# The opening of a hybrid decoder layer: the first tile's mean square and the factor of single tiles, written with fewer VectorE operations

## The chip, the cores and the metric

The kernel runs on one core of a Trainium2 chip. The time is device microseconds of one execution on that core; several executions are timed and their median is given. A profiled execution has a time of its own, and a span, which is the stretch from its first to its last instruction.

The engines are named as in the profile: PE (TensorE; PEld is its weight load), DVE (VectorE), ACT (ScalarE), POOL (GpSimd) and SP (SyncE, which mostly issues DMAs).

## The reference

One layer over 1024 tokens of width 1024, all in float32. What matters here is its first line, the RMS norm of the input, whose result feeds one wide projection:

```python
def rms_norm(x, w):
    xf = x.astype(jnp.float32)
    y = xf * lax.rsqrt(jnp.mean(xf * xf, axis=-1, keepdims=True) + EPS)
    return (y * w.astype(jnp.float32)).astype(x.dtype)

h = rms_norm(x, attn_norm_w[l])
proj = h @ w_in[l]                      # q, k, v, u, g
...                                     # differential attention, Conformer convolution, gated merge
x = x + (g_a * y_a + g_b * y_b) @ w_out[l]
h = rms_norm(x, ffn_norm_w[l])
gt, up = jnp.split(h @ w_gate_up[l], 2, axis=-1)
x = x + (jax.nn.silu(gt) * up) @ w_down[l]
```

For each token the norm needs one factor, 1/sqrt(mean of squares + 1e-6).

## The kernel before, in words

The tokens lie in eight tiles of 128 (`xt0` to `xt7`), one token to a partition. Every matrix product is made of three float32r products (high by high, low by high, high by low), so each operand is split into a high part by ACT (`split_hi`, line 120) and a low part by DVE (`split_lo`, line 125). The output of the norm is turned by PE (`turn_x`, line 724) and split into `hT_hi` and `hT_lo`, which stay for the whole first half of the kernel. The first products are those of the value projection (line 1110), for which a weight block `wraw` is loaded at the start and split into `vwh` and `vwl`.

The opening is written out by hand: a list of steps (line 1124 on), each of which is held in its place on DVE, ACT and PE by `in_order`. The steps are, in order: dummy products that keep PE busy, the squares of tile 0, its factor (`roots`), the spreading of the norm's gain over the partitions (`spread_weights`, PE line 212 and the two ACT copies of line 213), the scaling of tile 0 (`norm`, line 714), one more dummy product, the split of the first weight block, the turn of tile 0, the first products of tile 0, then squares, factor and scaling of tile 1, then those of tiles 2 and 3 together, and so on in pairs.

Tile 0 comes in two halves of 512 columns, the first by a DMA of the SP queue and the second by one of the ACT queue (line 202). Its squares are made in two places: ACT squares and sums the first half (line 699), DVE the second (line 700), and DVE adds the two sums (line 703). `rstd_of` (line 682) makes mean plus epsilon from the sum. `rsq` makes the factor: ACT takes the square root `t` of `v` (line 652), DVE its reciprocal `r` (line 653), and four DVE operations refine it by one Newton step, r(1.5 - 0.5 v r r) (lines 654 to 657). All of these are on one number per partition. Tile 1's factor is made alone as well; tiles 2 to 7 go in pairs, and the attention's norms, 16 numbers at a time, use the same function.

The small tiles come out of a pool named `sm`, which keeps a place per tag in the order in which tags first occur. The pools that are opened after it (the x tiles, the value splits, the attention's and the output projection's tiles of the left side of the memory) lie behind it.

Of the kernel before, what the change touches and what calls it, by code (L numbers as in the profile page):

```python
# [10 lines left out]
F32 = mybir.dt.float32  # L11
F32R = mybir.dt.float32r
AF = mybir.ActivationFunctionType
ALU = mybir.AluOpType
AX = mybir.AxisListType

P = 128
S = 1024
D = 1024
# [7 lines left out]
EPS = 1e-6  # L27
# [30 lines left out]
def kernel(  # L58
# [28 lines left out]
    dve, act, pool, pe = nc.vector, nc.scalar, nc.gpsimd, nc.tensor  # L87
# [11 lines left out]
    sm = ctx.enter_context(tc.tile_pool(name="sm", bufs=4))  # L99
# [12 lines left out]
    def nm(s):  # L112
        uid[0] += 1
        return f"{s}_{uid[0]}"
# [529 lines left out]
    def rsq(v, n, fast):  # L644

        r = sm.tile([P, 16], F32, tag="r", name=nm("r"))[:, :n]
        t = sm.tile([P, 16], F32, tag="t", name=nm("t"))[:, :n]
        if fast:
            act.activation(t, v, AF.Ln)
            act.activation(r, t, AF.Exp, scale=-0.5)  # L650
        else:
            act.activation(t, v, AF.Sqrt)
            dve.reciprocal(r, t)
        dve.tensor_tensor(t, r, r, op=ALU.mult)
        dve.scalar_tensor_tensor(t, v, 3.0e38, t, op0=ALU.min, op1=ALU.mult)
        dve.tensor_scalar(t, t, -0.5, 1.5, op0=ALU.mult, op1=ALU.add)
        dve.tensor_tensor(r, r, t, op=ALU.mult)
        return r
# [21 lines left out]
    def rstd_of(ss, n, scale, fast=False):  # L680
        v = sm.tile([P, 16], F32, tag="v", name=nm("v"))[:, :n]
        dve.tensor_scalar(v, ss, scale, EPS, op0=ALU.mult, op1=ALU.add)
        return rsq(v, n, fast)
# [3 lines left out]
    sqs = {}  # L687

    def squares(tiles):

        ss = sqs[tiles] = sm.tile([P, 4], F32, tag="ssx", name=nm("ssx"), bufs=2)[:, : len(tiles)]
        for j, i in enumerate(tiles):
            junk = ap.tile([P, D], F32, tag="junk", name=nm("xj"), bufs=1)
            src = xts[i]
            if i:
                act.activation(junk[:], src[:], AF.Square, accum_out=ss[:, j : j + 1])
            else:
                s2 = sm.tile([P, 1], F32, tag="ss", name=nm("ss"), bufs=1)
                act.activation(junk[:, :512], src[:, :512], AF.Square, accum_out=ss[:, j : j + 1])
                dve.tensor_tensor_reduce(  # L700
                    junk[:, 512:], src[:, 512:], src[:, 512:], 1.0, 0.0, ALU.mult, ALU.add, accum_out=s2[:]
                )
                dve.tensor_tensor(ss, ss, s2[:], op=ALU.add)

    def roots(tiles):

        r = rstd_of(sqs.pop(tiles), len(tiles), 1.0 / D)
        for j, i in enumerate(tiles):
            rx[i] = r[:, j : j + 1]

# [373 lines left out]
    def opening():  # L1084
# [35 lines left out]
        def turn_low(i):  # L1120
# [3 lines left out]
        steps(  # L1124
            lambda: keep_busy(3),
            lambda: squares((0,)),
            lambda: [xload(i, nc.scalar) for i in (2, 3)],
            lambda: roots((0,)),
            lambda: spread_weights(0),
            lambda: spread_weights(1),  # L1130
# [8 lines left out]
            lambda: low_x(0),  # L1139
            lambda: v_tile(0),  # L1140
            lambda: squares((1,)),
            lambda: roots((1,)),
            lambda: norm(1),
            lambda: squares((2, 3)),
            lambda: roots((2, 3)),
            lambda: turn_x(1),
            lambda: low_x(1),
# [88 lines left out]
    n = 0  # L1236
# [235 lines left out]
    n = len(steps)  # L1472
# [205 lines left out]
    for c in range(NE, NKT):  # L1678
        with after(mean_hi if c == NE else None), after(first_gates if c == NE else None):
            w = ws.next()  # L1680
# [465 lines left out]
```

## Time and profile before

| what | value |
|---|---|
| median of 3 runs | 1724.92 us (1724.23 to 1725.0) |
| profiled execution | 1724.03 us, span 1722.3 us |
| PE busy | 1713.7 us of the span |
| DVE busy | 1274.9 us |
| ACT busy | 873.3 us |
| POOL busy | 221.1 us |
| granted PE clock | 1.00 of full speed |
| start of the first product of the projection (line 1110) | 9.97 us into the span |

The profile's page gives shares over the whole span. The change lies in the first 17 us of it, so the timeline of the engines there says more: each of its rows has a start and a duration in us, the engine, the line of the kernel, what is written from what, the shape, how many instructions are merged in the row, and in brackets how long the engine had been idle and what released it. [...]

### The profile page before, as it was taken

To read this page: it belongs to the slowest core of one execution; us is meant where nothing else is said; L and a number is where in the kernel's file an instruction comes from. 1 tells how busy PE (TensorE), PEld (TensorE's weight loads), DVE (VectorE), ACT (ScalarE), POOL (GpSimd) and SP (SyncE) were. 2 spreads that over 40 slices of the span, in tenths; PEclk is the share of its full clock that TensorE was granted. 3 is DMA by queue.
4 is the path that set the end of the run, shared out by engine and by line. 5 is a ranking of instruction groups with operands and counts; after the bars stand their busy time and mean duration, and the time that the engine had idled before them with its cause. 6 is when DMAs were issued, how large, how long until landed. Compare 5 with 4: busy or idle time off the path is not lost.

```text
span 1722.3 us, 25855 instructions
## 1 busy us (share of the span) xinstructions
PE 1713.7 (100%) x9243; PEld 1478.0 (86%) x9243; DVE 1274.9 (74%) x2128; ACT 873.3 (51%) x1958; POOL 221.1 (13%) x211
## 2 busy tenths in 40 slices
PE   9999999999999999999999999999999999999999
PEld 7997889998998998988788888888888888888887
DVE  7675889898988987977577769966676666565544
ACT  5333335767877886856466325633333333333332
POOL 3997851000000000000000000000000000000000
PEclk9999999999999999999999999999999999999999
DMA  6344445436345445354873683244455445598663
GB/s 209 117 125 136 130 150 147 113 100 178 106 127 145 118 125 145 95 149 141 305 243 123 202 301 109 77 139 157 147 175 167 154 142 166 179 350 287 216 214 133
DMA packets 261347, 281.64 MB, mean 164 GB/s; under 512 B 16545, under 2 KB 181985, under 8 KB 261218
## 3 DMA queue, kind: packets, MB, share of 16 engines
q1 hardware_dynamic: 253584, 266.66, 48.3%
q0 software_dynamic: 6000, 10.43, 2.8%
q10 hardware_dynamic: 1634, 2.89, 0.5%
q8 instruction: 73, 1.20, 0.3%
q14 instruction: 56, 0.46, 0.1%
HBM read 181.84 MB, written 85.50 MB: 155 GB/s over the span
## 4 chain that ended last, share of the span: by engine, by line
PE 95%; DVE 2%; DMA 2%; ACT 1%; issue 0%; SPq 0%; DVEq 0%; ACTq 0%
PE acc L984 30%; PE pg L168 12%; PE acc L488 12%; PE pg L169 12%; PE pg L170 12%; PE wo L1861 3%; PE sc L1294 2%; PE sc L1293 2%; PE pT L1332 2%; DVE acc L594 1%; PE pg L1110 1%; PE pW L168 1%; PE pW L170 1%; PE pW L169 1%; PE pQ L819 1%; DMA room<-in_w_out_dram 1%
## 5 line engine op out<-in xcount | busy, mean ns | idle before, releaser
L594 DVE SCALAR_TENSOR_TENSOR acc<-u,cw,acc 128x1023 f32<-128x1023 f32 (+14 forms) x240 | 303.4, 1264 | 22.7 <-ACT acc L588 20.1
L168 PE MATMUL pg<-whi,hT_hi 128*128 128x256 f32 x704 | 199.3, 284 | 0.8 <-DVE v L125 0.8
L169 PE MATMUL pg<-wlo,hT_hi 128*128 128x256 f32 x704 | 199.9, 284 | 0.0
L170 PE MATMUL pg<-whi,hT_lo 128*128 128x256 f32 x704 | 199.9, 284 | 0.0
L125 DVE TENSOR_TENSOR wlo<-draw,whi 128x1024 fp32r<-128x1024 f32 x75 | 91.7, 1223 | 83.9 <-ACT whi L120 73.5
L120 ACT CAST whi<-draw 128x1024 fp32r<-128x1024 f32 x75 | 79.1, 1055 | 129.5 <-PE acc L488 112.7
L168 PEld LDWEIGHTS pg<-whi,hT_hi 128*128 128x128 f32 x704 | 133.8, 191 | 2.6 <-DVE v L125 1.0
L169 PEld LDWEIGHTS pg<-wlo,hT_hi 128*128 128x128 f32 x704 | 134.3, 191 | 1.7
L170 PEld LDWEIGHTS pg<-whi,hT_lo 128*128 128x128 f32 x704 | 134.3, 191 | 1.6
L120 ACT CAST whi<-wraw 128x1024 fp32r<-128x1024 f32 x90 | 94.6, 1052 | 67.2 <-PE pg L169 35.1
L488 PE MATMUL acc<-wlo,whi 128*128 128x512 f32 x308 | 119.8, 389 | 0.0
L488 PE MATMUL acc<-whi,wlo 128*128 128x512 f32 x308 | 119.8, 389 | 0.0
L168 PE MATMUL pg<-hT_hi,whi 128*128 128x512 f32 x288 | 114.5, 398 | 0.0
L169 PE MATMUL pg<-hT_lo,whi 128*128 128x512 f32 x288 | 113.9, 395 | 0.0
L170 PE MATMUL pg<-hT_hi,wlo 128*128 128x512 f32 x288 | 113.9, 395 | 0.0
L1300 ACT ACTIVATE E<-E,mn 128x640 f32<-128x640 f32 (+7 forms) x128 | 99.5, 777 | 26.6 <-DVE mn L1295 26.0
L120 ACT CAST whi<-s 128x1024 fp32r<-128x1024 f32 x54 | 56.8, 1053 | 105.2 <-PE acc L984 102.1
L125 DVE TENSOR_TENSOR wlo<-wraw,whi 128x1024 fp32r<-128x1024 f32 x75 | 93.2, 1246 | 16.3 <-ACT whi L120 15.8
L984 PE MATMUL acc<-h_hi,whi 128*128 128x512 f32 x240 | 93.4, 389 | 0.0
L984 PE MATMUL acc<-h_lo,whi 128*128 128x512 f32 x240 | 93.4, 389 | 0.0
L1295 DVE CUSTOM_DVE_ANT_0 E<-sc,tb 128x512 f32<-128x512 f32 (+3 forms) x128 | 74.1, 584 | 24.2 <-PE pT L1332 13.9
L984 PE MATMUL acc<-h_hi,wlo 128*128 128x512 f32 x240 | 90.1, 389 | 0.0
(372 smaller groups left out, 4593.1 us busy)
## 6 DMA issues: line engine op xcount, KB each, us to landing
wraw<-in_w_gate_up_dram SPq DMA_DIRECT2D x44, 512.0 KB, 4.7
wraw<-in_w_in_dram SPq DMA_DIRECT2D x38, 512.0 KB, 4.3
qs<-qs SPq DMA_DIRECT2D x96, 128.0 KB, 2.3
wd<-in_w_down_dram SPq DMA_DIRECT2D x44, 256.0 KB, 3.2
tdT<-wd SPq DMA_DIRECT2D x88, 128.0 KB, 4.5
draw<-sdS SPq DMA_DIRECT2D x44, 256.0 KB, 3.9
draw<-tdT SPq DMA_DIRECT2D x44, 256.0 KB, 3.5
wraw<-in_w_in_dram SPq DMA_DIRECT2D x32, 256.0 KB, 3.2
```

Of the source, the lines that this page charges most:

```text
L120: act.copy(dst, src)
L125: last_lo[0] = dve.tensor_tensor(dst, src, f32(hi), op=ALU.subtract).ins
L168: pe.matmul(o, lh, rh, start=start, stop=False)
L169: pe.matmul(o, lh, rl, start=False, stop=False)
L170: last_mm[0] = pe.matmul(o, ll, rh, start=False, stop=stop).ins
L488: m = pe.matmul(o[s_][i][:], l_[:, ts], r_[:, 512:], start=start and j + y_ == 0, stop=j == n - 1 and y_ == 2, skip_group_check=not start,)
L594: dve.scalar_tensor_tensor(a_, us[c][:, : S - n], cw[:, c, t : t + 1], a_, op0=ALU.mult, op1=ALU.add)
L984: last_mm[0] = pe.matmul(o[:], a_[x_][:, k, :], b_[y_][:, k, :], start=start and k + x_ + y_ == 0, stop=k == 3 and x_ == 1, skip_group_che ...
L1293: pe.matmul(o[:, :w], qh[:, qs], k, start=True, stop=False)
L1295: dve.tensor_tensor_reduce(e[:, ks], o[:, :w], tb[:, S - nk + c0 : S - nk + c0 + w], 1.0, mn[:, j : j + 1] if c0 else 3.0e38, ALU.add, ALU ...
L1300: act.activation(e[:, :nk], e[:, :nk], AF.Exp, bias=mn[:, j : j + 1], scale=-1.0, accum_out=l[:, j : j + 1])
L1861: last_mm[0] = pe.matmul(o[s_][i][:], A[u_], B[v_], start=start and j + y_ == 0, stop=j == 3 and y_ == 2, skip_group_check=not start,).ins
```

## The change

Two things are written with fewer DVE operations.

First, the mean square of tile 0. ACT's square now carries a scale of 1/sqrt(1024), so that its sum is a part of the mean; DVE adds epsilon to that; and the DVE operation that squares and sums the second half scales by 1/1024 and starts its sum from the value just made. What it leaves is `v` itself, the mean plus epsilon, so the addition of the two sums and the multiply-add of `rstd_of` are gone for this tile. The operation over the second half now reads the sum that ACT made of the first.

Second, the Newton step where one tile stands alone (tiles 0 and 1). A new small tile `w` holds -0.5 v; it is written between the issue of the square root and the reciprocal. Behind the reciprocal two operations are left: t = (r w) r and r = (t + 1.5) r.

```diff
@@ -650,7 +650,14 @@
         else:
             act.activation(t, v, AF.Sqrt)
+            if n == 1:
+                w = sm.tile([P, 1], F32, tag="w", name=nm("w"), bufs=1)
+                dve.tensor_scalar(w[:], v, 3.0e38, -0.5, op0=ALU.min, op1=ALU.mult)
             dve.reciprocal(r, t)
+            if n == 1:
+                dve.scalar_tensor_tensor(t, r, w[:], r, op0=ALU.mult, op1=ALU.mult)
+                dve.scalar_tensor_tensor(r, t, 1.5, r, op0=ALU.add, op1=ALU.mult)
+                return r
         dve.tensor_tensor(t, r, r, op=ALU.mult)
...
@@ -695,16 +702,18 @@
             else:
-                s2 = sm.tile([P, 1], F32, tag="ss", name=nm("ss"), bufs=1)
-                act.activation(junk[:, :512], src[:, :512], AF.Square, accum_out=ss[:, j : j + 1])
+                v = sm.tile([P, 16], F32, tag="v", name=nm("v"))[:, :1]
+                act.activation(junk[:, :512], src[:, :512], AF.Square, scale=D**-0.5, accum_out=ss[:, j : j + 1])
+                dve.tensor_scalar(ss, ss, EPS, None, op0=ALU.add)
                 dve.tensor_tensor_reduce(
-                    junk[:, 512:], src[:, 512:], src[:, 512:], 1.0, 0.0, ALU.mult, ALU.add, accum_out=s2[:]
+                    junk[:, 512:], src[:, 512:], src[:, 512:], 1.0 / D, ss, ALU.mult, ALU.add, accum_out=v
                 )
-                dve.tensor_tensor(ss, ss, s2[:], op=ALU.add)
+                sqs[tiles] = v

     def roots(tiles):

-        r = rstd_of(sqs.pop(tiles), len(tiles), 1.0 / D)
+        ss = sqs.pop(tiles)
+        r = rsq(ss, 1, False) if tiles == (0,) else rstd_of(ss, len(tiles), 1.0 / D)
```

On DVE the instructions of tile 0 stood like this before (`ss_350` is the sum of the second half, `ssx_348` that of the first, `xt_102` is tile 0; the two rows named ISA are one operation, the sum over the second half and the reading of its accumulator):

```order
L700 ISA xj_349,ss_350<-xt_102 128x512
L700 ISA ss_350 128x1
L703 TENSOR_TENSOR ssx_348<-ssx_348,ss_350 128x1
L682 TENSOR_SCALAR v_358<-ssx_348 128x1
L653 RECIPROCAL r_360<-t_361 128x1
L654 TENSOR_TENSOR t_361<-r_360 128x1
L655 SCALAR_TENSOR_TENSOR t_361<-v_358,t_361 128x1
L656 TENSOR_SCALAR t_361<-t_361 128x1
L657 TENSOR_TENSOR r_360<-r_360,t_361 128x1
L714 SCALAR_TENSOR_TENSOR xt_102<-xt_102,r_360,anw_b 128x512 x2
```

In the change they stand like this:

```order
L707 TENSOR_SCALAR ssx_348<-ssx_348 128x1
L708 ISA xj_349,v_350<-xt_102,ssx_348 128x512
L708 ISA v_350 128x1
L655 TENSOR_SCALAR w_361<-v_350 128x1
L656 RECIPROCAL r_358<-t_359 128x1
L658 SCALAR_TENSOR_TENSOR t_359<-r_358,w_361 128x1
L659 SCALAR_TENSOR_TENSOR r_358<-t_359,r_358 128x1
L723 SCALAR_TENSOR_TENSOR xt_102<-xt_102,r_358,anw_b 128x512 x2
```

Two small operations between the sum and the square root are gone, one has come ahead of the sum and one ahead of the reciprocal, and four behind the reciprocal have become two. For tile 1, alone too, `w` stands between the row of `v` and the reciprocal, and four operations become two in the same way. On DVE nothing else moves, and PE, ACT, POOL and SP have the same instructions in the same order as before.

One thing moves that is not an instruction. The tag "ss", under which the removed `s2` lay, is still used further on by `seen` (line 1183), so the pool `sm` keeps its place and gains one of 32 bytes per partition for `w`. In the built program everything that lies behind `sm` on the left side of the memory starts 32 bytes later: `xt0` at byte 164896 of its partition instead of 164864, and likewise the other x tiles, the splits of the value projection, the attention's tiles (`E`, `ph`, `pl`, `tb`, `early`) and the residual tiles `xa`. Before, these DMA targets started at multiples of 512 bytes. `hT_hi`, `hT_lo`, the weight tiles `wraw`, `whi`, `wlo` and everything on the right side of the memory stay where they were.

## The prediction

> **What bounds the kernel now.** I read the head of the page first, then the busy time by stretches (columns: length of the stretch, then each engine's busy time and instructions, clock, DMA share, GB/s).
>
> ```profile
> span 1722.3 us, 25855 instructions
> PE 1713.7 (100%) x9243; PEld 1478.0 (86%) x9243; DVE 1274.9 (74%) x2128; ACT 873.3 (51%) x1958; POOL 221.1 (13%) x211
> 0.00:16.00 16.00, 13.62 (x48) 8.83 (x48) 9.18 (x27) 10.30 (x19) 5.75 (x13) 1.00 0.81 279
> 16.00:60.00 44.00, 43.73 (x300) 39.86 (x299) 34.61 (x59) 19.06 (x34) 28.22 (x23) 1.00 0.43 127
> 812.00:825.00 13.00, 12.04 (x54) 8.92 (x53) 7.27 (x8) 10.02 (x23) 0.32 (x2) 1.00 0.71 218
> 1019.00:1024.00 5.00, 4.66 (x21) 3.56 (x20) 5.00 (x9) 1.33 (x5) 0.00 (x0) 1.00 1.05 406
> ```
>
> PE is idle for 8.6 us of the whole span (1722.3 - 1713.7). From 16 us on it is as good as full: 43.73 of the next 44 us. Only the first 16 us are not PE's: there it works on dummies and waits for the first normed tile. So what the opening gains reaches the end undiminished, if it still stands when PE becomes full at about 16 us, and nothing else in the kernel can gain. I therefore follow the opening instruction by instruction. DVE, tile 0:
>
> ```profile
> 4.84 0.69 DVE L700 CUSTOM_DVE_ANT_0 xj<-xt 128x512 f32<-128x512 f32 x1 [3.31 <-DMA xt<-in_x_dram]
> 5.46 0.08 DVE L700 DVE_READ_ACCUMULATOR2_ANT ss<- 128x1 f32 x1
> 5.65 0.16 DVE L703 TENSOR_TENSOR ssx<-ssx,ss 128x1 f32<-128x1 f32 x1
> 5.85 0.15 DVE L682 TENSOR_SCALAR v<-ssx 128x1 f32<-128x1 f32 x1
> 6.27 0.16 DVE L653 RECIPROCAL r<-t 128x1 f32<-128x1 f32 x1 [0.27 <-ACT t L652]
> 6.47 0.16 DVE L654 TENSOR_TENSOR t<-r 128x1 f32<-128x1 f32 x1
> 7.04 0.16 DVE L657 TENSOR_TENSOR r<-r,t 128x1 f32<-128x1 f32 x1
> 7.31 0.75 DVE L714 SCALAR_TENSOR_TENSOR xt<-xt,r,anw_b 128x512 f32<-128x512 f32 x1
> 7.98 0.74 DVE L714 SCALAR_TENSOR_TENSOR xt<-xt,r,anw_b 128x512 f32<-128x512 f32 x1
> ```
>
> The reader sees small operations of 0.16 us that follow each other at 0.20 us, since each needs the one before. What stands around them on ACT and PE:
>
> ```profile
> 3.60 0.63 ACT L699 ACTIVATE xj<-xt 128x512 f32<-128x512 f32 x1 [1.58 <-DMA xt<-in_x_dram]
> 4.14 0.19 ACT L699 ACTIVATION_READ_ACCUMULATOR xj<-xt 128x1 f32 x1
> 6.03 0.20 ACT L652 ACTIVATE t<-v 128x1 f32<-128x1 f32 x1 [1.71 <-DVE v L682]
> 5.75 1.06 PE L212 MATMUL pm<-anw_b,one 1*128 1x512 f32 x1
> 6.84 0.59 ACT L213 COPY anw_b<-pm 128x512 f32<-128x512 f32 x1
> 7.83 1.05 ACT L120 CAST vwh<-wraw 128x1024 fp32r<-128x1024 f32 x1 [0.40 <-DMA wraw<-in_w_in_dram]
> 8.21 1.94 PE L724 MATMUL px<-ident,xt 128*128 128x128 f32 x8 [0.65 <-DVE xt L714]
> 9.33 0.59 ACT L120 CAST hT_hi<-px 128x512 fp32r<-128x512 f32 x1 [0.45 <-PE px L724]
> 9.81 1.05 ACT L120 CAST vwh<-wraw 128x1024 fp32r<-128x1024 f32 x1
> ```
>
> **The change part by part.** *The epsilon ahead of the sum.* ACT's sum is read by 4.33 (4.14 + 0.19); the new addition, priced as the row at 5.85, ends at about 4.53 and is ready for its successor by about 4.6. DVE's half of the tile lands only at 4.84, so the addition is hidden by that DMA, with 0.2 us to spare. Were the cover gone, it would cost 0.2 us. *Between sum and root.* The accumulator is read by 5.54; the root started 0.03 us after the end of `v` (6.00 to 6.03), so it now starts at 5.57 and ends at 5.77. *`w`* takes the place that the addition had, 5.65 to 5.80, in DVE's idle time before the reciprocal, and is the last to let it go: reciprocal at 5.85, the two operations at 6.05 and 6.25, the scaling at 6.52 (0.27 behind, as from 7.04 to 7.31). That is 0.79 us earlier than 7.31.
>
> The sum and the first new operation read a per-partition number as an operand, which the trace shows only in the large rows: 0.75 with one (line 714) against 0.69 for the sum without. So 0.06 each, if size does not matter, or nothing: 0.67 to 0.79; I take 0.7, nearer neither end. ACT's scale I cost at nothing; its square ends 0.2 us clear anyway.
>
> *What catches the gain.* Three things stand on the path next. The second scaling needs the second ACT copy, which starts when PE ends its product (5.75 + 1.06 = 6.81) and ends at 7.43 as before; so it runs at about 7.47 instead of 7.98 and keeps 0.5. PE's first turn follows the first scaling, and its four transposes end at 8.6 instead of 9.3. But ACT's cast of the weight block waits for its DMA, not for us: it runs from 7.83 to 8.88 as before, and the cast of `hT_hi` comes behind it, at 8.88 instead of 9.33 (0.45), or 0.1 earlier if ACT overlaps the two as it does at 9.81. So about 0.5 us is left behind tile 0. ACT works without a gap from there to tile 1's squares, so all of them move by that. I take it that the second weight block and tiles 1 to 3 have landed by then; no wait shows when they do.
>
> Tile 1, and tiles 2 and 3:
>
> ```profile
> 10.94 2.38 POOL L1137 TENSOR_TENSOR vwl<-wraw,vwh 128x1024 fp32r<-128x1024 f32 x1 [9.64 <-ACT vwh L120]
> 12.43 0.15 DVE L682 TENSOR_SCALAR v<-ssx 128x1 f32<-128x1 f32 x1 [0.36 <-ACT xj L696]
> 12.85 0.16 DVE L653 RECIPROCAL r<-t 128x1 f32<-128x1 f32 x1 [0.27 <-ACT t L652]
> 13.05 0.29 DVE L654 TENSOR_TENSOR t<-r 128x1 f32<-128x1 f32 x1
> 13.95 0.75 DVE L714 SCALAR_TENSOR_TENSOR xt<-xt,r,anw_b 128x512 f32<-128x512 f32 x1
> 14.86 0.19 ACT L696 ACTIVATION_READ_ACCUMULATOR xj<-xt 128x1 f32 x1
> 15.28 0.16 DVE L682 TENSOR_SCALAR v<-ssx 128x2 f32<-128x2 f32 x1
> 15.59 1.17 ACT L120 CAST hT_hi<-px 128x512 fp32r<-128x512 f32 x2
> 16.21 1.35 PE L1110 MATMUL pg<-vwh,hT_hi 128*128 128x256 f32 x8
> ```
>
> Tile 1 has two operations fewer (0.39), one with the dearer operand: 0.33 to 0.39. The row of 0.29 ends with POOL's (13.34 and 13.32): the DVE operation was held by it. POOL starts behind ACT's second weight cast and moves by the same 0.5, so the first new operation is held about as long. Tile 1's scaling thus comes 0.5 + 0.35 = 0.85 earlier. Then the squares of tile 3 limit: they are read by 15.05, less 0.5 is 14.55, so `v` of the pair stands at 14.6 instead of 15.28, the root and the cast 0.65 earlier, and PE's row at 16.21 likewise. From there PE is full. **The sum** is 0.65 us by this way, 0.45 if only ACT's gap counts, 0.85 if squares and landings give way too. I take 0.6.
>
> Against the profiled execution that is 1724.03 - 0.6 = 1723.4 (1.7 us lie around its span). The median of the runs shown stands 0.9 above it, so I predict 1724.92 - 0.6 = 1724.3 us. A difference of 0.2% is 3.45 us, about what a measurement of this kernel can tell from no change; the gain is a sixth of that.
>
> *The memory that moves.* 32 bytes more in the small pool shift x tiles, `early` and `xa` off their multiples of 512. No row shows what a DMA pays for such a start in this memory. Three of these transfers lie on the chain that ended last (start, us):
>
> ```profile
> 1.31 3.51 DMA xt<-in_x_dram
> 812.34 7.69 DMA early<-a_d
> 1013.29 5.10 DMA xa<-in_x_dram
> wd<-in_w_down_dram SPq DMA_DIRECT2D x44, 256.0 KB, 3.2
> draw<-tdT SPq DMA_DIRECT2D x44, 256.0 KB, 3.5
> u<-u_d SPq DMA_DIRECT2D x8, 512.0 KB, 4.4
> tb<-t_d SPq DMA_DIRECT2D x8, 512.0 KB, 4.2
> ```
>
> They sum to 16.3 us, so each per cent costs 0.16 us. Bounds: `tb` reads rows 4604 bytes apart, whose starts in the source fall anywhere, and lands no later than the aligned `u` (4.2 against 4.4): nothing, or even a gain of 5% (0.8 us), which I leave aside as scatter. `draw` starts 256 bytes past a multiple of 512 and `wd` on one: 9% longer, 1.5 us. I take nothing, since `tb` is the nearer case, and keep 1.5 for the range.
>
> [...]
>
> **The rivals.** *Swallowed:* the weight block, the gain's copy or a landing of tiles 1 to 3 takes what the factor gives. For it: ACT's wait for `wraw` stands right there, and DMA is busy 0.81 of the first 16 us. Against it: ACT was idle 0.45 us before `hT_hi`. Time: 1724.9 less 0 to 0.3, 1724.7. *Serial sum, slower:* before, the two halves were squared side by side; now DVE's sum waits for ACT's. It has 0.2 us to spare only because the SP half lands 1.2 us ahead (3.60 and 4.84). If both landed at 4.84, ACT's sum would be read at 5.57, epsilon added at 5.77, and DVE would start at 5.88, 1.04 later, against 0.7 saved: 0.3 slower, 1725.2. It decides from a lead below some 0.3 us. *Moved memory, slower:* transfers to the shifted tiles take longer. It cancels the gain from 4% (0.65 us); at 9% the time is 1724.3 + 1.5 = 1725.8; for 0.2% it would take 25%, for which no row speaks. *It does more:* the full 0.85, 1724.0. *It does not do what it says* is excluded: the built order has the operations named.
>
> **How the numbers follow.** Forecast 0.52; swallowed 0.20; moved memory 0.13; serial sum 0.07; more 0.08. The range takes in the forecast, the larger gain with the scatter of the three runs (1724.0 less 0.7), and the moved memory's 1725.8: 1723.3 to 1725.8. All cases lie within 0.2%; I leave 0.05 for transfers that are far dearer than any row (slower) and 0.02 for the reverse.
>
> **What would show it.** In the profile after, tile 0's first scaling at 6.5 to 6.65, the second at 7.47, the cast of `hT_hi` right behind the weight cast, tile 1's scaling near 13.1 and PE's row of 16.21 at 15.5 to 15.8. Wrong I would be if DVE's sum started after 4.84 (or its DMA), if ACT waited for a landing between 8.9 and 14, or if PE showed new idle time near 812 or 1019 behind `early` or `xa`.

## The result and the profile after

The changed kernel takes 1727.41 us (median of 22 runs, 1726.16 to 1729.16) against 1724.64 us (22 runs, 1723.21 to 1725.64) for the kernel before: a ratio of 1.0017, 95% interval 1.0011 to 1.0022. It is slower by 2.8 us. That lies outside the predicted range and, by 0.7 us, inside the bound of 0.2%. Both profiled executions fit: 1727.22 us after, 1724.03 before. A ratio compares all runs of two kernels; it is not the quotient of the medians beside it.

The head of the page, then the busy time by stretches as shown of before:

```profile
span 1725.4 us, 25852 instructions
PE 1717.1 (100%) x9243; PEld 1478.0 (86%) x9243; DVE 1275.1 (74%) x2125; ACT 873.0 (51%) x1958; POOL 221.2 (13%) x211
0.00:16.00 16.00, 13.94 (x50) 9.41 (x51) 9.52 (x28) 10.83 (x20) 6.26 (x15) 1.00 0.86 292
16.00:60.00 44.00, 43.90 (x301) 40.08 (x301) 33.96 (x55) 19.14 (x33) 28.40 (x21) 1.00 0.43 123
812.00:825.00 13.00, 12.20 (x61) 9.36 (x61) 6.33 (x7) 9.85 (x22) 0.54 (x3) 1.00 0.78 246
1019.00:1024.00 5.00, 4.61 (x21) 3.48 (x19) 4.27 (x7) 0.32 (x2) 0.00 (x0) 1.00 1.05 402
```

The span is 3.1 us longer and PE is busy 3.4 us longer, with the same 9243 products. PE's idle time is 8.3 us where it was 8.6. The time went into PE's own work, not into a wait. The opening, meanwhile, did what was forecast. DVE in the timeline of after, with two rows of ACT and one of PE:

```profile
4.26 0.15 DVE L707 TENSOR_SCALAR ssx<-ssx 128x1 f32<-128x1 f32 x1 [2.74 <-ACT xj L706]
5.06 0.75 DVE L708 CUSTOM_DVE_ANT_0 xj<-xt,ssx 128x512 f32<-128x512 f32 x1 [0.64 <-DMA xt<-in_x_dram]
5.85 0.15 DVE L655 TENSOR_SCALAR w<-v 128x1 f32<-128x1 f32 x1
5.85 0.20 ACT L652 ACTIVATE t<-v 128x1 f32<-128x1 f32 x1 [1.62 <-DVE v L708]
6.09 0.16 DVE L656 RECIPROCAL r<-t 128x1 f32<-128x1 f32 x1
6.29 0.22 DVE L658 SCALAR_TENSOR_TENSOR t<-r,w 128x1 f32<-128x1 f32 x1
6.54 0.16 DVE L659 SCALAR_TENSOR_TENSOR r<-t,r 128x1 f32<-128x1 f32 x1
6.80 1.41 DVE L723 SCALAR_TENSOR_TENSOR xt<-xt,r,anw_b 128x512 f32<-128x512 f32 x2
8.82 0.58 ACT L120 CAST hT_hi<-px 128x512 fp32r<-128x512 f32 x1
13.06 1.41 DVE L723 SCALAR_TENSOR_TENSOR xt<-xt,r,anw_b 128x512 f32<-128x512 f32 x2
15.72 1.23 PE L1119 MATMUL pg<-vwh,hT_hi 128*128 128x256 f32 x8 [0.24 <-ACT hT_hi L120]
```

From the start of the sum to the first scaling it takes 1.74 us (6.80 - 5.06) where it took 2.47 (7.31 - 4.84): 0.73 saved. In this execution the tile's second half landed 0.22 us later than in the one of before.

Where the time is lost shows in the answer for the line of the products that are made from sums of quarters of their matrices (line 984 before, 993 after). They come in two stretches: a part of the wide projection from 110 to 250 us, and the feed-forward's first product from 1100 to 1520. PE is full there, in both kernels: busy 140.00 us of the 140 and 420.00 of the 420. The columns are count, duration in ns (least, median, greatest), and the start of the first and of the last of them in us. `T1h` to `T4l` are such sums of the normed input, high and low parts, 512 columns at a time, which PE multiplies by weights of 128 x 128 from `whi`, `wlo`, `sh` or `sl`. Before:

```profile
L984 PE MATMUL acc<-hT_hi,whi x83: 387/389/496, 112.0 to 245.9; 128*128 128x512 f32 x83
L984 PE MATMUL acc<-T1h,whi x28: 389/389/389, 116.8 to 238.8; 128*128 128x512 f32 x28
...
L984 PE MATMUL acc<-T4h,sh x80: 389/389/389, 1151.6 to 1513.1; 128*128 128x512 f32 x80
```

After:

```profile
L993 PE MATMUL acc<-hT_hi,whi x83: 387/389/499, 111.3 to 247.7; 128*128 128x512 f32 x83
L993 PE MATMUL acc<-T1h,whi x28: 393/396/399, 116.1 to 240.5; 128*128 128x512 f32 x28
...
L993 PE MATMUL acc<-T4h,sh x80: 392/395/396, 1153.0 to 1516.2; 128*128 128x512 f32 x80
```

The first of the 28 products `T1h` by `whi` starts 0.7 us earlier than before, the last 1.7 us later: 2.4 us are lost between them. Between the first and the last `T4h` by `sh` of the second stretch another 1.6 to 1.7 us go. Each such product lasts 395 to 396 ns where it lasted 389, and from the start of one to the start of the next it is about 234 ns where it was 227 (worked out from all starts in the traces). The products of `hT_hi` by `whi`, in between them, last 389 as before.

The kinds that pay are those of the first stretch with `T1` to `T4` (12 kinds of 28, 336 products: 336 x 7 ns = 2.35 us) and those of the second with `sh` and `sl` (3 kinds of 80: 240 x 7 ns = 1.68 us). That is 4.0 us less 0.7 gained at the start: 3.3, against 3.1 in the span.

Where these tiles lie in the built programs fits the pattern. The `T` tiles of the first stretch and the `sh`, `sl` of the second moved by 32 bytes (`T1h` from 172544 to 172576, `sh` from 135680 to 135712). `hT_hi`, `whi`, `wlo`, the `T` tiles of the second stretch and the `sh`, `sl` of the first are where they were. Of the products of 512 columns, the kinds that pay are exactly those with one operand that moved and one that did not.

### The profile page after: what moved, and what is told of

Same layout as the page of the kernel before. It is cut to its first block, busy times and chain, and to the rows that moved or that the text cites. A ratio compares the mean times of both kernels' runs of the same rounds, so it can differ in the third digit from the quotient of the medians.

```text
span 1725.4 us, 25852 instructions
## 1 busy us (share of the span) xinstructions
PE 1717.1 (100%) x9243; PEld 1478.0 (86%) x9243; DVE 1275.1 (74%) x2125; ACT 873.0 (51%) x1958; POOL 221.2 (13%) x211
## 4 chain that ended last, share of the span: by engine, by line
PE 94%; DMA 2%; DVE 2%; ACT 1%; issue 0%; SPq 0%; ACTq 0%
PE acc L993 30%; PE acc L488 12%; PE pg L168 12%; PE pg L169 12%; PE pg L170 12%; PE wo L1870 3%; PE sc L1303 2%; PE sc L1302 2%; PE pT L1341 2%; PE pg L1119 1%; DVE acc L594 1%; PE pW L168 1%; PE pW L170 1%; PE pW L169 1%; PE pQ L828 1%; DMA room<-in_w_out_dram 1%
## 5 line engine op out<-in xcount | busy, mean ns | idle before, releaser
L120 ACT CAST whi<-draw 128x1024 fp32r<-128x1024 f32 x75 | 79.1, 1055 | 129.6 <-PE acc L488 111.1
```

Source lines behind the costliest of these rows:

```text
L120: act.copy(dst, src)
```

## Experiments

The theory formed on this: a product of 512 columns takes about 7 ns longer when its two operands do not start at the same place within some block of memory. The rivals: the loss comes from the new operations or the new tile, or it comes from where one operand lies by itself, the moved tiles no longer starting at a multiple of 64 or 128. A pool's unused tile `pad_sm` lies ahead of the small tiles, so its size moves what lies behind without an instruction. The expectations name the theories by letters: A is the first, counted within 64 bytes; B says that any operand off a multiple of 64 costs; C that only multiples of 256 or 512 count, later that the distance within 256 does; D is that of the new operations.

**The move alone**: the kernel before, moved by 32 bytes.

```diff
-    sm.tile([P, 32], F32, name="pad_sm", bufs=1)
+    sm.tile([P, 40], F32, name="pad_sm", bufs=1)
```

> The kernel before with 32 bytes more in the small pool and no operation changed; every tile that the change moved now lies exactly where the change puts it. Theory A (the product's operands, moved by 32 bytes, cost about 7 ns in each product of 512 columns of lines 984): slower than before by 3.8 us, 1728.4 us, with the 12 groups of T products between 110 and 250 us and the three of sh and sl after 1100 us at 395 instead of 389 ns. Theory D (the new operations or their waits disturb what follows): as before, 1724.6 us.

Measured: 1727.9 us (11 runs) against 1724.24 (27 runs), ratio 1.0022 [1.0013, 1.0030]. The same two kinds of product:

```profile
L984 PE MATMUL acc<-T1h,whi x28: 393/396/399, 117.4 to 241.7; 128*128 128x512 f32 x28
...
L984 PE MATMUL acc<-T4h,sh x80: 392/395/396, 1153.5 to 1516.8; 128*128 128x512 f32 x80
```

The move costs 3.7 us without any change to an operation. The first stretch is 124.3 us long (241.7 - 117.4) where it was 122.0, the second 363.3 where it was 361.5.

**The operations alone**: the change, but `w` takes the place of the tag "ss", so that nothing behind it moves.

```diff
-                w = sm.tile([P, 1], F32, tag="w", name=nm("w"), bufs=1)
+                w = sm.tile([P, 1], F32, tag="ss", name=nm("w"), bufs=1)
```

> The change with w under the tag that s2 had, so that nothing in the memory moves. Theory A: the opening's gain alone, 0.7 us faster than before, 1723.9 us, and all T products at 389 ns. Theory D: as the change, 1727.4 us.

Measured: 1723.95 us (11 runs), ratio 1.0003 [0.9993, 1.0013]. All products with `T` tiles are back at 389 ns. So the loss of the change is the move. Whether the operations gain is not settled by this run: its median is 0.3 us below before, while two of its runs (1728.84 and 1731.79) raise the mean. In its profiled execution PE was 0.5 us ahead behind the opening and lost 0.9 us at 224 us, where it waited 0.59 us for the `wlo` that POOL makes; the change itself shows no such wait there.

**Moved by 64, 128 and 256 bytes.** The first is the change with `pad_sm` 32 bytes larger, the other two are the operations alone with it 128 and 256 bytes larger (64 and 96 floats).

```diff
-    sm.tile([P, 32], F32, name="pad_sm", bufs=1)
+    sm.tile([P, 96], F32, name="pad_sm", bufs=1)
```

> The change with another 32 bytes in the small pool, so that the moved tiles lie 64 bytes off their old places. If the place within 64 bytes counts (theories A and B): 1723.9 us, as without any move, T products at 389 ns. If multiples of 256 or 512 bytes count (theory C, the transfers or the products): as the change, 1727.4 us or more.

> The change's operations, w in the old tag, and the tiles behind the small pool moved by 128 bytes. Where weights and moving operand start 32 or 64 bytes apart within 256 a product of 512 columns took 4 to 7 ns more; 256 bytes apart (late T with whi, before) it took none. If only an offset of a full 256 counts as none: T products of the first part and late sh, sl products at 391 to 396 ns, 2 to 3.7 us slower than without the move, 1726 to 1727.5 us. If 128 is harmless already: 389 ns and 1723.9 us.

> The same with a move by 256 bytes. If the two operands' places within 256 bytes count: no cost, products at 389 ns, 1723.9 us as without the move. If multiples of 512 are needed: as the change, about 1727 us.

Measured: 64 bytes 1726.98 us, ratio 1.0015 [1.0007, 1.0024]; 128 bytes 1728.0 us against 1725.06, ratio 1.0012 [1.0002, 1.0022]; 256 bytes 1723.63 us, ratio 0.9988 [0.9978, 0.9997]. One run of before, of 1732.29 us, lowers the last two ratios; without it the means stand at 1.0016 and 0.9992. The same kinds, moved by 64 bytes:

```profile
L993 PE MATMUL acc<-T1h,whi x28: 388/394/398, 116.6 to 240.1; 128*128 128x512 f32 x28
...
L993 PE MATMUL acc<-T4h,sh x80: 393/396/398, 1152.6 to 1516.3; 128*128 128x512 f32 x80
```

Moved by 128:

```profile
L993 PE MATMUL acc<-T1h,whi x28: 387/394/398, 116.2 to 240.3; 128*128 128x512 f32 x28
...
L993 PE MATMUL acc<-T4h,sh x80: 392/394/404, 1151.8 to 1515.6; 128*128 128x512 f32 x80
```

Moved by 256:

```profile
L993 PE MATMUL acc<-T1h,whi x28: 389/389/389, 115.7 to 237.7; 128*128 128x512 f32 x28
...
L993 PE MATMUL acc<-T4h,sh x80: 389/389/389, 1151.0 to 1512.5; 128*128 128x512 f32 x80
```

A multiple of 64 or of 128 is not enough, and the theories that ask for no more than that fall. At 256 the cost is gone. The place within 256 bytes is what counts.

**Nearly the whole left side moved by 32**, in the kernel before: now `hT_hi`, `whi` and the first stretch's `T` tiles lie alike again, all 32 bytes off a multiple of 256, while the right side stays.

```diff
-    cst.tile([P, 16], F32, name="pad_left")
+    cst.tile([P, 24], F32, name="pad_left")
```

> The kernel before with 32 bytes more at the start of the left side of the memory: hT, the weight splits whi and wlo, and all that lies behind them move by 32 bytes together; the right side stays. Theory A (it counts that weights and moving operand start at different places within 64 bytes): T products of the first part, both operands moved, stay at 389 ns; products that take one operand from either side become 395 ns (aT with whi, late T1 to T3 with whi, late T4 with sh, mT with whi, early T4 with sh, about 1570 of them): 10 us slower, 1735 us. Theory B (any operand off a multiple of 64 bytes costs): all products of 512 columns on hT, h2, cT and the weight splits too, some 4700: 30 us slower, 1755 us.

Measured: 1736.12 us (5 runs, 1735.55 to 1737.21), ratio 1.0070 [1.0056, 1.0084]: 11.9 us slower. By the addresses in the built program 1620 products of 512 columns now have their operands 32 bytes apart; at 7 ns each that is 11.3 us. Products of the first stretch with `whi`, of which both operands moved, products of the second with `whi`, of which one did, and those of the output projections (`aTl` on the right side, `cT_lo` on the left):

```profile
L984 PE MATMUL acc<-T1h,whi x28: 389/389/396, 117.4 to 240.6; 128*128 128x512 f32 x28
...
L984 PE MATMUL acc<-T1h,whi x80: 395/396/397, 1139.0 to 1512.7; 128*128 128x512 f32 x80
...
L169 PE MATMUL pg<-aTl,whi x128: 392/395/497, 822.7 to 916.9; 128*128 128x512 f32 x128
L169 PE MATMUL pg<-cT_lo,whi x128: 389/389/395, 917.6 to 1004.5; 128*128 128x512 f32 x128
```

Where both operands moved, nothing is paid although neither starts at a multiple of 256 any more. Where one moved, the product pays: `T1h` by `whi` free in the first stretch and dear in the second, the mirror image of the change. `aTl` by `whi` lasted 389 before, and its 128 products took 92.3 us from first to last start (819.8 to 912.1) where they now take 94.2; `cT_lo` by `whi`, both moved, takes 86.9 us in both. So it is the distance of two operands that counts, not the place of either. Products of 256 columns with one operand moved (`vwh` by `hT_hi`) stayed at 117 to 120 ns from start to start.

**The unit matrix at a multiple of 256**, with the operations alone: it begins 192 bytes behind one in the kernel before and in the change (224 where the left side is moved by 32), and is the moving operand of all transposes.

```diff
+    neglam = cst.tile([P, 1], F32, name="neglam")
+    lsum = cst.tile([P, 2], F32, name="lsum")
     ident = cst.tile([P, P], F32, name="ident")
```

> The operations alone without the move, and two small tiles (neglam, lsum) taken ahead of ident, so that the unit matrix begins at byte 16640, a multiple of 256, where it began 192 bytes behind one at 16576. It is the moving operand of the transposes of 128 columns (109 ns from start to start, 480 of them and more), whose weights begin at multiples of 256. Theory C with the limit that the run of the left side moved by 32 showed (products of 256 and 128 columns do not pay): transposes stay at 109 ns, 1723.2 to 1724.8 us. Rival (the transposes pay already, in the kernel before): 5 to 8 ns less each, 500 of them, 2.5 to 4 us less: 1720 to 1722 us.

Measured: 1723.49 us against 1724.59 (11 and 27 runs), ratio 0.9994 [0.9985, 1.0003]; the transposes stay at 109 ns from start to start. These products of 128 columns do not pay for their place, and nothing is to be had there.

**The change whole, put back and moved by 256**: `w` under its own tag, and `pad_sm` smaller by those 32 bytes (24 floats), or larger by 224 (88 floats).

```diff
-    sm.tile([P, 32], F32, name="pad_sm", bufs=1)
+    sm.tile([P, 24], F32, name="pad_sm", bufs=1)
```

> The change whole, with w under its own tag, and the unused tile pad_sm made 32 bytes smaller (96 bytes where it was 128), so that the T tiles, sh and sl begin again where they began before (172544, 147968, 135680). Theory C as it now stands (it counts how far apart within 256 bytes the weights' and the moving operand's tiles begin): the T products back at 226 to 227 ns from start to start, no loss at 110 to 250 and 1100 to 1515 us, and the opening's gain of 0.7 us is left under the scatter of the landing of tile 0: 1723.2 to 1724.8 us, median near 1724.0. Rival (the loss comes from the new tile or the operations on it, not from where the others lie): 1726.5 to 1728, as the change itself.

> The change whole, and pad_sm made 224 bytes larger, so that with w's 32 bytes everything behind it lies 256 bytes further than before. Theory C as it now stands: the same as the change put back, 1723.2 to 1724.8 us, T products at 226 to 227 ns. Rival (256 bytes further is better than the places of before, as the one run moved by 256 with 0.9988 might be read): about 2 us under the run of before and 1 us or more under the change put back. Rival (a multiple of 256 was not what helped that run, but its tile w under the tag ss): 1726.5 to 1728.

Measured: put back 1723.15 us, a hair under the range expected, ratio 0.9993 [0.9985, 1.0002]; moved by 256 1723.71 us, ratio 0.9994 [0.9985, 1.0003]. The change put back:

```profile
L993 PE MATMUL acc<-T1h,whi x28: 389/389/389, 115.9 to 237.9; 128*128 128x512 f32 x28
...
L993 PE MATMUL acc<-T4h,sh x80: 389/389/389, 1150.3 to 1511.8; 128*128 128x512 f32 x80
```

Eight floats less in an unused tile give back what the change lost: PE is 0.9 us ahead of before at both ends of the first stretch and 1.3 at both ends of the second. It is also not better than the same at 256 bytes, so the run moved by 256 above was not faster for its place. Five kernels have the operations and pay for no place; their ratios are 1.0003, 0.9988, 0.9993, 0.9994 and 0.9994, in the mean 0.9994, or 1.0 us. Only one of the five intervals leaves out 1, by itself a weak result. The last three, though (the unit matrix and the two of this section), were timed side by side against the same 27 runs of before. Taken together their 33 runs stand 1.0 us below it in the mean, 0.7 to 1.4 at 95% (worked out from the single times), so a gain of the operations is shown, of the size that the opening gives. Against the change itself the change put back is clearly faster, as their intervals (0.9985 to 1.0002, and 1.0011 to 1.0022) do not touch.

**Each half of the change by itself**, with nothing moved: the sum alone (the Newton step as before), and the Newton step alone (the sum as before).

> The first part of the change alone (mean plus epsilon in one go), nothing moved. By the prediction's steps from DVE's start of the sum to the first scaling: 2.47 us before, less 0.39 for two operations, plus up to 0.06 for the pointer: 2.08 to 2.14 us. If the part is hidden by the root's or the copies' waits: 2.47.

> The second part alone (the factor in three operations), nothing moved. From DVE's start of the sum to the first scaling: 2.47 us before, less 0.39, plus up to 0.06: 2.08 to 2.14 us; tile 1's way from its v to its scaling 1.52 us before, 1.13 to 1.19 with the part. If w delays the reciprocal: 0.1 more each.

Measured, DVE in the timeline, the sum alone:

```profile
5.73 0.75 DVE L701 CUSTOM_DVE_ANT_0 xj<-xt,ssx 128x512 f32<-128x512 f32 x1 [1.21 <-DMA xt<-in_x_dram]
...
7.80 0.75 DVE L716 SCALAR_TENSOR_TENSOR xt<-xt,r,anw_b 128x512 f32<-128x512 f32 x1
```

The Newton step alone:

```profile
4.79 0.69 DVE L707 CUSTOM_DVE_ANT_0 xj<-xt 128x512 f32<-128x512 f32 x1 [3.26 <-DMA xt<-in_x_dram]
...
6.93 1.41 DVE L721 SCALAR_TENSOR_TENSOR xt<-xt,r,anw_b 128x512 f32<-128x512 f32 x2
```

From sum to scaling 2.07 and 2.14 us, against 2.47 with neither and 1.74 with both: 0.40 and 0.33, together the 0.73. Tile 1 gains from the second part too: in the Newton step alone 1.15 us pass from its `v` to its scaling (12.05 to 13.20), before 1.52. The single times of the two, 1723.37 and 1722.89 us, cannot tell them apart.

**What the opening is worth at the first stretch.** Two rows of each profile, the start of DVE's sum and the first `T1h` by `whi`, separate the operations from the landing:

| kernel | sum starts | first `T1h` by `whi` | difference |
|---|---|---|---|
| before | 4.84 | 116.8 | 111.96 |
| move alone | 5.37 | 117.4 | 112.03 |
| left side moved by 32 | 5.62 | 117.4 | 111.78 |
| sum alone | 5.73 | 117.3 | 111.57 |
| Newton step alone | 4.79 | 116.2 | 111.41 |
| the change | 5.06 | 116.1 | 111.04 |
| operations alone | 5.26 | 116.3 | 111.04 |
| moved by 256 | 4.64 | 115.7 | 111.06 |
| change put back | 4.88 | 115.9 | 111.02 |

The sum starts anywhere between 4.64 and 5.73 us, as the DMA lands it, with 1.1 us between the ends. What it loses there, PE loses at 116 us. Past the landing the kernels with both parts agree to 0.1 (the four not listed have 111.0 to 111.1). They gain 0.9 us against before and the move alone, 0.4 by the sum and 0.55 by the Newton step; against the left side moved, which has the operations of before as well, it is 0.7, and why that one stands 0.2 lower is open.

## Why the prediction was wrong

*What bounds the kernel.* PE full from 16 us on was right, and a gain in the opening did reach the first stretch undiminished. "Nothing else in the kernel can gain" was the half of it that misled: the same fullness means that a product that takes longer is paid at once, and 576 products by 7 ns, 4.0 us, outweigh an opening of 0.9 us.

*The opening.* Its steps held. The epsilon addition was hidden (4.26 to 4.41, and the sum waited 0.64 us for its DMA), `w` stood where it was put, though the root, which ended at 6.05, and not `w`, which ended at 6.00, let the reciprocal go at 6.09; the two operands per partition cost 0.06 us each (0.75 for 0.69, 0.22 for 0.16), and 0.73 us were saved of the 0.67 to 0.79 forecast. ACT's cast of `hT_hi` came at 8.82, right behind the weight cast that ends at 8.89 (the two rows overlap by 0.07), tile 1's scaling at 13.06 (forecast near 13.1), PE's row of 16.21 at 15.72 (forecast 15.5 to 15.8). The sum was undersized: 0.6 was taken for all of it and the runs show 0.9. The short term is the half microsecond that was to be left behind tile 0: from the start of the sum to the cast of `hT_hi` it is 3.76 us (8.82 - 5.06) where it was 4.49 (9.33 - 4.84), so all of the 0.73 was left, and tile 1's part came on top. The rival *it does more*, with 0.85, had the size. The profiled execution kept 0.7 of it, since its tile landed 0.2 us late.

*Swallowed* and *serial sum* did not occur. PE was ahead throughout the first 110 us. In the profile after, though, the weight block was as late as tile 0: the chain that ended last begins there with `1.71 6.11 DMA wraw<-in_w_in_dram`, where it began with `xt` before, so a further gain would have had the weight block in its way. In no run did ACT's half set the start of DVE's sum; the DMA did each time, by 0.24 us at the least.

*The memory that moves: "I take nothing".* This is the step that failed, and not by its size: it priced the wrong user of the memory and left the right one at nothing. It looked for the cost in the DMAs that write to the moved tiles, and the rival's 1725.8 was the dearest of these. In the profile after, two steps of the chain of waits and two groups of transfers:

```profile
813.86 7.42 DMA early<-a_d
1014.59 5.12 DMA xa<-in_x_dram
...
xa<-in_x_dram SPq DMA_DIRECT2D x16, 256.0 KB, 5.3
xt<-in_x_dram SPq DMA_DIRECT2D x4, 512.0 KB, 4.9
```

On the chain `early` took 7.42 us for 7.69 and `xa` 5.12 for 5.10; in the groups `xa` took 5.3 us for 5.2 and `xt` 4.9 for 5.2 (5.9 in the move alone, with the same places: so much do these landings scatter). No dearer transfer is seen, and no new idle time near 812 or 1019. A price of the new starts below the scatter of these landings could not be seen: no run here shows one, and none speaks against it. What did pay were PE's products on the moved tiles. The prediction names the moved tiles of the DMAs and leaves out that the `T`, `sh` and `sl` tiles had moved as well and are operands of 576 products, each of which then took about 7 ns more, 4.0 us in all. No row of the trace before could have given the price, since there all these pairs lie alike. It could have shown how many products have one operand on each side of the move, and that 6 ns on each would cost the 0.2% that the text held to need a DMA 25% longer.

*The chances.* 0.93 for within 0.2% was too sure. The outcome of 0.17% lies within it by luck: it came through a mechanism for which there was no case, its interval reaches 0.22%, and the time lies 1.6 us above the top of the range.

## What to carry to other kernels

A new small tile in a pool moves every tile behind it, here by 32 bytes. Where matrix products of 512 columns fill PE, compare in the built program where both operands of each lie, before and after, and keep them alike within 256 bytes (227 ns each here, and about 234 where they were 32 bytes apart); an unused tile that is shrunk by as much costs nothing (the change put back: ratio 0.9993). When an edit is worth less than a microsecond, test the edit and its effect on the memory's layout apart from the start, and measure a gain in an opening past the landing that starts it.

## What the runs showed of the hardware

In these kernels a 128x512 float32r product in a full PE takes 227 ns from start to start when its weights and its moving operand start at the same place within 256 bytes. The medians by kind are 232 to 235 ns when they start 32 bytes apart, 228 to 233 at 64 and 231 to 236 at 128, and 227 again when they are 256 bytes apart or moved together. Products of 256 and 128 columns showed no such cost where one operand moved (117 to 120 and 109 ns). Half of 227 is 113.5; a cost of up to 6 ns, by this estimate, could be hidden in the 120 of a product of 256 columns. The place is not the only thing that makes a product of 512 columns longer: those of the attention's scores stood at 232 to 233 ns in the kernels compared, with both tiles at multiples of 256.

Why this is so is open. The load of a product's weights overlaps the product ahead of it, as these two rows of before show (the load starts 0.2 us ahead of its product and lasts 188 ns):

```profile
L984 PEld LDWEIGHTS acc<-T1h,whi x108: 187/188/188, 116.6 to 1500.0; 128*128 128x128 f32 x108
L984 PE MATMUL acc<-T1h,whi x108: 389/389/389, 116.8 to 1500.2; 128*128 128x512 f32 x108
```

A guess of the author's is that it is the weights loaded meanwhile that have to lie like the moving operand of the product that runs. The starts of single products speak for it in part. In the change's second stretch the product just ahead of each group with `sh` and `sl` has operands that lie alike and still takes 235 ns, in all 20 groups (226 to 227 before): while it runs, the moved `sh` is loaded (from 231 to 233 ns ahead of its own product on, for 187 to 188). With the left side moved by 32, the last product of a group of `T4` in the first stretch has operands 32 bytes apart and takes 226 to 227 ns in five cases of six: the weights loaded meanwhile lie like its moving operand. But the last product of a group in the change's second stretch takes 232 to 234 ns, and moved by 64 the product ahead of the group takes 225 to 226; neither fits. So the guess is not shown: no run took the overlap away. Whether the 7 ns grow with the columns above some length was not tried either.
